# A two-layer trunk with eight experts: every second expert piece started by GpSimd's DMA queue, an over-capacity branch placed earlier, and the first pieces put in other tiles

## The chip, the cores and the metric

One core of a Trainium2 chip runs the whole program. The metric is the device time in microseconds (us) of one execution. The kernel before takes 1315.39 us (median of three runs, 1314.02 to 1319.24).

## The reference

A sequence of 256 tokens of width 1024 goes through two residual layers, each with two sub-layers of the form x <- LayerNorm(ALPHA * x + sublayer(x)). The first layer has a convolution and pooling mixer and a dense SwiGLU, the second a gated convolution with spatial gating and a top-2-of-8 expert SwiGLU. All tensors are float32. What matters here is the last sub-layer:

```python
def moe_swiglu(x, router, w_gate, w_up, w_down):
    t = x.reshape(-1, d)
    logits = (t @ router).astype(jnp.float32)
    top_logits, top_idx = lax.top_k(logits, TOP_K)          # 2 of 8
    top_w = jax.nn.softmax(top_logits, axis=-1)
    gates = jnp.sum(jax.nn.one_hot(top_idx, N_EXPERTS) * top_w[..., None], axis=1)
    out = jnp.zeros_like(t)
    for e in range(N_EXPERTS):
        out = out + gates[:, e:e + 1] * swiglu(t, w_gate[e], w_up[e], w_down[e])
    return out.reshape(bsz, s, d)
```

Each expert has w_gate and w_up of 1024 x 3584 and w_down of 3584 x 1024, so the eight experts are 352 MB of weights, all of which are read.

## The kernel before

**Pieces.** All large weights are cut into pieces (`chunks`) of 1 MiB each, in the order in which they are used. 57 pieces belong to the two layers' other matrices, 336 to the experts; this text counts the expert pieces from 0 to 335, so that piece m is chunk 57 + m. A piece is 512 rows of 512 columns for gate and up (2 KB runs) and 256 rows of 1024 columns for down (4 KB runs). The function `raw_half` starts a piece's DMA; it is called for half a piece at a time, ahead of its use, by `prep`. Every one of these DMAs is issued by SyncE (SP), at lines 123, 131, 133 and 136, in the order of the pieces.

**Tiles.** Normally a piece lands in one of eight `raw` tiles, which go round. A DMA waits in its queue until the last reader of its tile is done, and what stands behind it in the same queue waits too. For the first 60 expert pieces the table `AHEAD` gives further places: tiles of the earlier layers that are free by then ("fd" from piece 15 to 24, for instance; "fd" last holds the gains `rows` of the odd layer's first LayerNorm, which `affine` reads at lines 524 and 525). `IN_HI` and `IN_LO` put certain pieces in the tiles of the `hip` and `lop` pools, which otherwise hold converted halves: pieces 16 to 18 in `whi` and 19 and 20 in `wlo`, and, counted from the end, pieces 329 to 331 in `whi` and 332 and 333 in `wlo`.

**Passes.** The experts are ranked by their number of tokens, and eight passes p run over them, with room for 64, 160, 128, 128, 64, 64, 64 and 64 tokens (`CAPS`); pass 0 is always expert 0, the expert of the others is read into a register (`value_load`) once it is known. A pass has seven blocks f, each of a gate, an up and a down item; `plan` lists the 168 items of all passes, and an item uses two pieces. A narrow item (64 tokens) multiplies with the float32 piece as it landed. A wide item first splits each half into a rounded part (`whi`, ScalarE, line 151) and a rest (`wlo`, VectorE, line 158), from `hip` (6 tiles) and `lop` (5). Passes 0 alone, then 0 and 2, 2 and 6, 1 with 6, 4 and 5, 5 and 3, 3 and 7, and at last 7 alone run interleaved.

**The branch.** If an expert has more tokens than its room, `over_capacity` computes the rest in a loop; with these inputs the branch isn't taken. It stands `IF_AT` = 5 items before the last item (item 162, whose first piece is 324). Ahead of it `drain` works off all deferred steps, and `raw_half` starts all pieces that are left. SP, TensorE, ScalarE and VectorE have instructions in the branch, and each of them waits behind it for its own semaphores to reach the values that the branch leaves (line 1463).

**GpSimd's queue.** In program order behind the earlier layers' work it holds two DMAs of `rows` (line 529, for the tile "fd"), four multiplications `total` (line 1083), the branch, and two DMAs `lnf` of 512 KB each (line 1540). Expert piece 0 is started in program order ahead of `rows`, all others behind it.

**The end.** Item 167 uses pieces 334 and 335, whose DMAs are cut in two (`LAST_CUT`). Behind it stand the last combination, a LayerNorm and the store.

Of the kernel before, what the change touches and what calls it, by code (L numbers as in the profile page):

```python
# [8 lines left out]
F32 = mybir.dt.float32  # L9
# [8 lines left out]
P = 128  # L18
T = 256
# [4 lines left out]
NE = 8  # L24
# [8 lines left out]
RAW_BUFS = 8  # L33
WAIT = (6, 12, 6, 2)
CARRY = {(1, 0): 1, (1, 1): 2, (0, 0): 3, (0, 1): 3}
IF_AT = 5
CARRY_AT = 1
LAST_CUT = 2
AHEAD = {"ft": (0, 50), "fd": (15, 24), "fa": (2, 18), "fc": (3, 48), "fe": (7, 50), "fb": (8, 56), "f0": (9, 18), "f1": (10, 60)}

IN_HI, IN_LO = (16, 17, 18, -7, -6, -5), (19, 20, -4, -3)
TAIL, TAIL_HI, TAIL_LO = 12, 2, 1
RANK_AT = 3
FILL = (5, 2, 5, 4)
# [31 lines left out]
def tile_trunk(ctx: ExitStack, tc: tile.TileContext, a: dict, out: bass.AP, caps=CAPS, starts=STARTS,  # L76
               stop=None, dump=None):
    nc = tc.nc
    te, ve, se, pe_, sy = nc.tensor, nc.vector, nc.scalar, nc.gpsimd, nc.sync
# [21 lines left out]
    chunks, slot_pools = [], {"ra": rawp}  # L101
# [9 lines left out]
    def block_chunk(w, r0, c0):  # L111
        chunks.append((lambda: w[r0:r0 + 512, c0:c0 + 512].rearrange("(k p) f -> p k f", p=P), 4, 512))

    def raw_half(n):

        c, h = divmod(n, 2)
        src, k, f = chunks[c]
        if c in ahead and ahead[c] in ("whi", "wlo"):
            if c not in raws:
                pool = hip if ahead[c] == "whi" else lop  # L120
                raws[c] = [pool.tile([P, k // 2, f], F32, name=ahead[c]) for _ in range(2)]
                for i, r in enumerate(raws[c]):
                    sy.dma_start(r, src()[:, i * k // 2:(i + 1) * k // 2, :])
            return raws[c][h]
        if c not in raws:
            tag = ahead.get(c, "raw")
            raws[c] = slot_pools[tag[:2]].tile([P, k, f], F32, name="raw", tag=tag)
            v = src()
            if c < FIRST_CUT:
                for i in range(2):  # L130
                    sy.dma_start(raws[c][:, :, i * P:(i + 1) * P], v[:, :, i * P:(i + 1) * P])
            elif c < len(chunks) - LAST_CUT:
                sy.dma_start(raws[c], v)
            else:
                for i in range(2):
                    sy.dma_start(raws[c][:, i * k // 2:(i + 1) * k // 2, :], v[:, i * k // 2:(i + 1) * k // 2, :])
        return raws[c][:, :, h * P:(h + 1) * P] if k == DB else raws[c][:, h * k // 2:(h + 1) * k // 2, :]

    spare = []
# [59 lines left out]
    eid_reg = {}  # L199
# [61 lines left out]
        plan.insert(len(plan) - 2, plan.pop(len(plan) - 5))  # L261

    def expert(p, w, r0, nr, c0, ncol):
        def src():
            if p and p not in eid_reg:
                eid_reg[p] = sy.value_load(ctli[0:1, p:p + 1], min_val=0, max_val=NE - 1)
            if p == 0:
                v = w[0, r0:r0 + nr, c0:c0 + ncol]
            else:
                v = w[bass.ds(eid_reg[p], 1), r0:r0 + nr, c0:c0 + ncol].rearrange("o r f -> (o r) f")  # L270
            return v.rearrange("(k p) f -> p k f", p=P)
        chunks.append((src, nr // P, ncol))

# [8 lines left out]

    for tag, cs in (("whi", IN_HI), ("wlo", IN_LO)):
        for c in cs:
            ahead[c + (n_moe // 2 if c > 0 else len(chunks))] = tag

    def stay_warm(n, w, m=None):

# [1170 lines left out]
    def over_capacity():  # L1459
# [3 lines left out]
        with tc.If(flag > 0):  # L1463
# [15 lines left out]
            for e in range(NE):  # L1479
                with tc.For_i(0, FE, P) as f0:  # L1480
# [6 lines left out]
                    for i in range(2):  # L1487
                        for k in range(DB):
                            mm(bs[i][:, :T], wgu[:, i, k, :], xf[:, k, :], k == 0, k == DB - 1)
                    s = mop.tile([P, T], F32, name="fbh", tag="mh", bufs=2)  # L1490
                    se.activation(s, bs[0][:, :T], AF.Silu)
                    ve.tensor_tensor(s, s, bs[1][:, :T], op=OP.mult)
                    for t in range(2):
# [15 lines left out]
    for n, item in enumerate(plan):  # L1509
# [5 lines left out]
            later(1, gather, *gathers[item])  # L1515
        if n == end - IF_AT:
            drain()
            for c in range(made["hi"] // 2, len(chunks)):
                raw_half(2 * c)
            over_capacity()  # L1520
        if n == end - CARRY_AT:
# [93 lines left out]
```

## Time and profile before

| | |
|---|---|
| median of three runs | 1315.39 us |
| the profiled execution | 1314.88 us |
| its span in the trace | 1313.2 us |
| TensorE busy | 1256.2 us (96%) |
| VectorE, ScalarE, GpSimd busy | 713.5, 514.5, 32.0 us |
| moved by DMA | 421.17 MB, mean 321 GB/s |
| hardware queue, software queue | 414.58 MB, 5.28 MB |

Busy time of TensorE is modelled and isn't a measure of how close it is to its peak. The software queue is GpSimd's, the hardware queue SP's. "DMA share" in the views is the busy share of the 16 DMA engines; since packets overlap, it goes a little over 1.

### The profile page before, as it was taken

The numbers are of one execution on the slowest core, as the hardware profiler recorded it, in microseconds if no ns is written. First come the engines' busy times: TensorE is split into PE (matmuls) and PEld (weight loads), VectorE is DVE, ScalarE is ACT, GpSimd is POOL, SyncE is SP. The second block draws the span as 40 slices with busy tenths as digits, with TensorE's granted clock in tenths as the row PEclk, the third lists the DMA queues.
The fourth block names the chain that finished last, engine by engine and source line by source line (L and its number), as shares of the span: only waits on it lengthen the run. The fifth ranks groups of instructions, "written<-read, shape, count | busy, mean of one in ns | idle before, by whom it ended". The sixth has DMA issues, their size and how long they took to land. (4 is left out here: it accounts for less than half of the span.)

```text
span 1313.2 us, 19384 instructions
## 1 busy us (share of the span) xinstructions
PE 1256.2 (96%) x7585; PEld 871.1 (66%) x7585; DVE 713.5 (54%) x1105; ACT 514.5 (39%) x726; POOL 32.0 (2%) x69
## 2 busy tenths in 40 slices
PE   7989999999999999999999999999999999999875
PEld 6848888888777666667765566565556567665541
DVE  4897676667984244655534334434435565564313
ACT  4246555546442144544432233332333244454200
POOL 5000000001000001000000000000000000000000
PEclk8999999999999999999999999999999999999988
DMA  8425755176875999999999999999999999999991
GB/s 293 166 70 176 256 184 182 65 253 194 323 271 185 393 393 394 394 392 393 393 393 371 381 397 374 364 380 391 392 397 396 394 393 395 393 394 394 393 393 76
DMA packets 195884, 421.17 MB, mean 321 GB/s; under 512 B 6896, under 2 KB 43448, under 8 KB 195784
## 3 DMA queue, kind: packets, MB, share of 16 engines
q1 hardware_dynamic: 194280, 414.58, 85.2%
q0 software_dynamic: 1504, 5.28, 1.1%
q8 instruction: 61, 1.00, 0.3%
q14 instruction: 39, 0.32, 0.1%
HBM read 418.78 MB, written 1.05 MB: 320 GB/s over the span
## 5 line engine op out<-in xcount | busy, mean ns | idle before, releaser
L158 DVE TENSOR_TENSOR wlo<-raw,whi 128x1024 fp32r<-128x1024 f32 x354 | 417.8, 1220 | 175.8 <-ACT whi L151 159.1
L151 ACT ACTIVATE whi<-raw 128x1024 fp32r<-128x1024 f32 x354 | 354.6, 1050 | 215.7 <-DMA raw<-in_odd_moe_w_up 99.1
L98 PE MATMUL mm<-whi,xgw 128*128 128x512 f32 x672 | 215.9, 403 | 0.4 <-DVE total L1431 0.4
L98 PEld LDWEIGHTS mm<-whi,xgw 128*128 128x128 f32 x672 | 122.0, 189 | 44.6 <-issue 13.3
L98 PE MATMUL mm<-raw,f1k 128*64 128x256 f32 (+1 forms) x1344 | 133.9, 384 | 0.0
L98 PE MATMUL mm<-wlo,xgw 128*128 128x512 f32 x336 | 131.9, 392 | 0.3 <-DVE wlo L158 0.3
L98 PE MATMUL mm<-big,whi 128*128 128x512 f32 (+1 forms) x448 | 129.2, 368 | 2.5 <-ACT whi L151 1.8
L98 PE MATMUL mm<-raw,fek 128*64 128x256 f32 x880 | 106.6, 390 | 7.3 <-DVEq L1463 6.7
L98 PE MATMUL acc<-whi,mh 128*128 128x512 f32 x336 | 106.3, 397 | 1.7 <-ACT whi L151 1.7
L98 PEld LDWEIGHTS mm<-raw,f1k 128*64 128x64 f32 (+1 forms) x1344 | 72.7, 127 | 52.2 <-issue 17.4
L1298 ACT ACTIVATE fdk<-mm 128x256 f32<-128x256 f32 (+1 forms) x49 | 23.2, 474 | 182.1 <-PE mm L98 181.9
L98 PE MATMUL mm<-big,wlo 128*128 128x256 f32 x384 | 92.7, 283 | 0.0
L98 PEld LDWEIGHTS mm<-raw,fek 128*64 128x64 f32 x880 | 61.1, 139 | 45.5 <-issue 19.0
L1301 DVE TENSOR_TENSOR fdk<-mm,fdk 128x256 f32<-128x256 f32 (+1 forms) x49 | 26.3, 537 | 118.5 <-PE mm L98 118.5
L98 PEld LDWEIGHTS mm<-big,whi 128*128 128x128 f32 x448 | 74.9, 192 | 14.2 <-ACT whi L151 2.0
L98 PE MATMUL acc<-raw,fbs 128*64 128x512 f32 (+1 forms) x528 | 84.0, 507 | 0.0
L98 PEld LDWEIGHTS acc<-whi,mh 128*128 128x128 f32 x336 | 61.4, 188 | 24.4 <-ACT whi L151 11.0
L98 PEld LDWEIGHTS mm<-wlo,xgw 128*128 128x128 f32 x336 | 63.5, 189 | 14.9 <-DVE wlo L158 0.7
L98 PEld LDWEIGHTS mm<-big,wlo 128*128 128x128 f32 x384 | 69.3, 192 | 3.7
L98 PE MATMUL acc<-wlo,mh 128*128 128x512 f32 (+1 forms) x176 | 67.8, 401 | 0.5 <-DVE wlo L158 0.5
L98 PEld LDWEIGHTS acc<-raw,fbs 128*64 128x64 f32 (+1 forms) x528 | 26.6, 125 | 47.9 <-issue 44.9
L98 PE MATMUL acc<-whi,ffh 128*128 128x512 f32 x176 | 55.6, 396 | 0.0
(292 smaller groups left out, 1315.7 us busy)
## 6 DMA issues: line engine op xcount, KB each, us to landing
raw<-in_odd_moe_w_gate SPq DMA_DIRECT2D x110, 1024.0 KB, 13.8
raw<-in_odd_moe_w_up SPq DMA_DIRECT2D x109, 1024.0 KB, 13.9
raw<-in_odd_moe_w_down SPq DMA_DIRECT2D x105, 1024.0 KB, 12.8
raw<-in_even_ffn_w_gate SPq DMA_DIRECT2D x11, 1024.0 KB, 5.6
raw<-in_even_ffn_w_up SPq DMA_DIRECT2D x11, 1024.0 KB, 8.3
raw<-in_even_ffn_w_down SPq DMA_DIRECT2D x11, 1024.0 KB, 7.0
raw<-in_odd_w_in SPq DMA_DIRECT2D x10, 1024.0 KB, 15.2
raw<-in_even_w_in SPq DMA_DIRECT2D x5, 1024.0 KB, 8.8
```

Source lines behind the costliest of these rows:

```text
L98: te.matmul(o, lhsT, rhs, start=start, stop=stop)
L151: se.activation(his[n], r, AF.Copy)
L158: ve.tensor_tensor(los[n], r, his[n].bitcast(F32), op=OP.subtract)
L1298: se.activation(s, v, AF.Silu)
L1301: ve.tensor_tensor(s, v, s, op=OP.mult)
```

## The change

Five edits:

- A new function `raw_queue` gives the issuing engine of a piece: GpSimd for every second chunk of the experts, SP for the others. Since 57 chunks come before, GpSimd gets the expert pieces 0, 2, 4, ..., 334 and SP 1, 3, ..., 335. An item's two pieces so have one queue each. The register with the expert's number is loaded on both engines.
- `IF_AT` goes from 5 to 10: the branch stands before item 157 (piece 314).
- Ahead of the branch only pieces up to eight behind the present one are started, no longer all that are left; and no piece of the end goes to `whi` or `wlo` any more.
- At the start, pieces 15 to 17 go to `whi`, 18 and 19 to `wlo`, and 20 to "fd" (before: 15 to "fd", 16 to 18 to `whi`, 19 and 20 to `wlo`).
- A tile inside the branch has another tag ("sgate" in place of "mh").

```diff
-IF_AT = 5
+IF_AT = 10
-AHEAD = {"ft": (0, 50), "fd": (15, 24), ...
-IN_HI, IN_LO = (16, 17, 18, -7, -6, -5), (19, 20, -4, -3)
+AHEAD = {"ft": (0, 50), "fd": (20, 24), ...
+IN_HI, IN_LO = (15, 16, 17), (18, 19)
...
+    def raw_queue(c):
+
+        return pe_ if c >= n_moe // 2 and c % 2 else sy
...
+                v = src()
                 for i, r in enumerate(raws[c]):
-                    sy.dma_start(r, src()[:, i * k // 2:(i + 1) * k // 2, :])
+                    raw_queue(c).dma_start(r, v[:, i * k // 2:(i + 1) * k // 2, :])
...
             elif c < len(chunks) - LAST_CUT:
-                sy.dma_start(raws[c], v)
+                raw_queue(c).dma_start(raws[c], v)
...
     def expert(p, w, r0, nr, c0, ncol):
+        on = raw_queue(len(chunks))
+
         def src():
-            if p and p not in eid_reg:
-                eid_reg[p] = sy.value_load(ctli[0:1, p:p + 1], min_val=0, max_val=NE - 1)
+            if p and (p, on) not in eid_reg:
+                eid_reg[p, on] = on.value_load(ctli[0:1, p:p + 1], min_val=0, max_val=NE - 1)
...
-            ahead[c + (n_moe // 2 if c > 0 else len(chunks))] = tag
+            ahead[n_moe // 2 + c] = tag
...
-                    s = mop.tile([P, T], F32, name="fbh", tag="mh", bufs=2)
+                    s = mop.tile([P, T], F32, name="fbh", tag="sgate", bufs=1)
...
-            for c in range(made["hi"] // 2, len(chunks)):
+            for c in range(made["hi"] // 2, state["use"] // 2 + RAW_BUFS):
                 raw_half(2 * c)
             over_capacity()
```

## Rows read from the trace of the kernel before

**Rows 1.** Windows of the streaming stage: busy us (instructions) per engine, granted clock, DMA share, GB/s.
```profile
430.00:460.00 30.00, 30.00 (x212) 18.11 (x209) 8.01 (x12) 6.13 (x9) 0.00 (x0) 1.00 1.04 393
...
1100.00:1200.00 100.00, 99.99 (x554) 67.36 (x550) 55.56 (x61) 44.80 (x54) 0.00 (x0) 1.00 1.04 393
```
**Rows 2.** Waits: engine, tile, line, released by: us in total, times, longest.
```profile
ACT whi L151 <- DMA raw<-in_odd_moe_w_up: 99.1, 33, 9.8
```
**Rows 3.** Windows around the start of the expert stage.
```profile
380.00:390.00 10.00, 9.84 (x43) 7.64 (x42) 7.70 (x19) 1.26 (x3) 0.00 (x0) 1.00 1.01 374
390.00:400.00 10.00, 10.00 (x68) 8.85 (x67) 6.31 (x25) 4.98 (x11) 0.00 (x0) 1.00 0.83 314
400.00:410.00 10.00, 10.00 (x80) 8.23 (x79) 5.40 (x25) 3.09 (x7) 0.00 (x0) 1.00 0.00 0
410.00:420.00 10.00, 10.00 (x92) 6.47 (x92) 6.66 (x17) 1.16 (x3) 0.00 (x0) 1.00 0.51 185
```
**Rows 4.** Timeline of SP's DMA queue there: start us, us, what, count.
```profile
343.93 1.64 SPq L133 DMA_DIRECT2D raw<-in_odd_moe_w_up  x2
...
384.77 29.32 SPq L133 DMA_DIRECT2D raw<-in_odd_moe_w_down  x2
414.18 2.09 SPq L123 DMA_DIRECT2D whi<-in_odd_moe_w_gate  x4
```
**Rows 5.** Timeline of VectorE and TensorE: last readers of the tiles.
```profile
413.00 0.69 DVE L525 TENSOR_TENSOR tok<-tok,rows 128x512 f32<-128x512 f32 x1
402.78 0.72 PE L98 MATMUL acc<-whi 128*128 128x512 f32 x2
```
**Rows 6.** Timeline of GpSimd.
```profile
304.15 0.77 POOL L901 DMA_DIRECT2D fc<-in_odd_sgu_w  x1
...
375.62 0.56 POOL L529 DMA_DIRECT2D rows<-in_odd_ln_g  x1 [61.11 <-DVE big L436]
...
509.92 5.89 POOL L1083 TENSOR_SCALAR total<-tok 128x512 f32<-128x512 f32 x4 [133.21 <-DVE wlo L158]
992.51 0.59 POOL L1540 DMA_DIRECT2D lnf<-in_odd_ln_g  x1 [476.70 <-PE mm L98]
```
**Rows 7.** Timeline of TensorE and ScalarE: the first items of the expert stage.
```profile
406.94 2.81 PE L98 MATMUL mm<-raw,xg 128*64 128x256 f32 x24
448.69 3.89 ACT L151 ACTIVATE whi<-raw 128x1024 fp32r<-128x1024 f32 x4
...
462.17 3.89 ACT L151 ACTIVATE whi<-raw 128x1024 fp32r<-128x1024 f32 x4
```
**Rows 8.** Page, DMA issues: count, KB each, median us to landing.
```profile
raw<-in_odd_moe_w_gate SPq DMA_DIRECT2D x110, 1024.0 KB, 13.8
```
**Rows 9.** One window and one VectorE instruction beside GpSimd's DMAs.
```profile
990.00:1000.00 10.00, 10.00 (x85) 6.62 (x84) 3.65 (x9) 0.98 (x2) 1.12 (x2) 1.00 1.04 391
375.37 1.22 DVE L158 TENSOR_TENSOR wlo<-raw,whi 128x1024 fp32r<-128x1024 f32 x1
```
**Rows 10.** Windows in which the DMA rate sinks.
```profile
700.00:800.00 100.00, 96.50 (x706) 58.58 (x707) 40.91 (x52) 29.68 (x38) 0.00 (x0) 1.00 1.02 383
800.00:900.00 100.00, 99.22 (x718) 60.48 (x718) 40.45 (x51) 31.22 (x43) 0.00 (x0) 1.00 1.00 373
```
**Rows 11.** The branch: TensorE's loads behind it, SP's semaphores behind it, a window.
```profile
1268.22 0.32 PEld L98 LDWEIGHTS mm<-raw,fek 128*64 128x64 f32 x4 [7.15 <-issue]
L1463 SPq EVENT_SEMAPHORE  x8: 17/17/17, 1282.6 to 1286.8; - x8
1260.00:1270.00 10.00, 3.25 (x17) 1.80 (x15) 1.49 (x3) 0.39 (x1) 0.00 (x0) 0.81 1.05 390
```
**Rows 12.** TensorE's last item.
```profile
1293.39 3.60 PE L98 MATMUL acc<-raw,fbs 128*64 128x512 f32 x16
```
**Rows 13.** Page, DMA queues: packets, MB, share of 16 engines' span.
```profile
q1 hardware_dynamic: 194280, 414.58, 85.2%
q0 software_dynamic: 1504, 5.28, 1.1%
```

More of the change, by code (lines that the diff above doesn't have):

```diff
@@ L35 @@
 CARRY = {(1, 0): 1, (1, 1): 2, (0, 0): 3, (0, 1): 3}
-IF_AT = 5
+IF_AT = 10
 CARRY_AT = 1
 LAST_CUT = 2
-AHEAD = {"ft": (0, 50), "fd": (15, 24), "fa": (2, 18), "fc": (3, 48), "fe": (7, 50), "fb": (8, 56), "f0": (9, 18), "f1": (10, 60)}
-IN_HI, IN_LO = (16, 17, 18, -7, -6, -5), (19, 20, -4, -3)
+AHEAD = {"ft": (0, 50), "fd": (20, 24), "fa": (2, 18), "fc": (3, 48), "fe": (7, 50), "fb": (8, 56), "f0": (9, 18), "f1": (10, 60)}
+IN_HI, IN_LO = (15, 16, 17), (18, 19)
 TAIL, TAIL_HI, TAIL_LO = 12, 2, 1
@@ L132, in raw_half @@
             elif c < len(chunks) - LAST_CUT:
-                sy.dma_start(raws[c], v)
+                raw_queue(c).dma_start(raws[c], v)
             else:
                 for i in range(2):
-                    sy.dma_start(raws[c][:, i * k // 2:(i + 1) * k // 2, :], v[:, i * k // 2:(i + 1) * k // 2, :])
+                    raw_queue(c).dma_start(raws[c][:, i * k // 2:(i + 1) * k // 2, :],
+                                           v[:, i * k // 2:(i + 1) * k // 2, :])
         return raws[c][:, :, h * P:(h + 1) * P] if k == DB else raws[c][:, h * k // 2:(h + 1) * k // 2, :]
@@ L269, in src @@
             else:
-                v = w[bass.ds(eid_reg[p], 1), r0:r0 + nr, c0:c0 + ncol].rearrange("o r f -> (o r) f")
+                v = w[bass.ds(eid_reg[p, on], 1), r0:r0 + nr, c0:c0 + ncol].rearrange("o r f -> (o r) f")
             return v.rearrange("(k p) f -> p k f", p=P)
```

## The prediction, before the changed kernel ran

> **What bounds the kernel now.** First the windows. From 430 to about 1283 us the DMA engines are busy without a gap (share 1.04) and move 393 GB/s [rows 1]. An expert piece of 1.049 MB so takes 2.67 us, and 336 of them 897 us, most of the span. The waits say the same from the reader's side: ScalarE's conversion of up pieces alone waited 33 times, 99 us in all, for a DMA [rows 2]. So in this stage time is bytes over rate, and a change gains only by moving bytes into stretches where the engines idle, by closing a hole in the stream, or by shortening what follows the last byte. The views that matter are therefore the two ends of the stream and its holes.
>
> **The start.** Between 380 and 420 us the rate is 374, 314, 0 and 185 GB/s [rows 3]. Against 393 these four windows leave (19 + 79 + 393 + 208) / 393 x 10 = 17.8 us unused. SP's queue shows why: its down pieces 14 and 15 begin at 384.77 and fill the time to 414.1, and only at 414.18 come the `whi` pieces [rows 4]. Piece 15 goes into "fd", whose last reader is the `affine` that ends at 413.00 + 0.69 = 413.69 us [rows 5]; pieces 16 to 20 stand behind it in the queue though their tiles are free sooner.
>
> In the change pieces 15 to 19 need `whi` and `wlo` tiles only. The last reader of those is the warming matmul that ends at 402.78 + 0.72 = 403.5 us [rows 5], most others are done before. So up to five pieces, 13.3 us of transfers, can run in the unused stretch, and only piece 20 waits for 413.69, on GpSimd, with SP's odd pieces free to go on.
>
> Something is given back. GpSimd has piece 0 and then, in program order, the two `rows` DMAs, which waited for their tile until 375.62 [rows 6]; all other even pieces stand behind them. SP now begins pieces 2 and 3 at 343.93 and 4 and 6 behind them, well ahead of 14 at 384.77 [rows 4]; in the change 2, 4 and 6 start about 377, three pieces x 2.67 = 8.0 us that move into the stretch. They are still in time: TensorE begins piece 0 at 406.94 [rows 7], 30 us later. Net 17.8 - 8.0 = **9.8 us** more of the stream is done by 420.
>
> It counts only if TensorE can keep up. From piece 0 (406.94) to the first conversion, piece 24 (448.69), it takes 1.74 us a piece, and from piece 24 to piece 30 (462.17) 13.48 / 6 = 2.25 us [rows 7]; both are under 2.67. The lead of 9.8 us on the DMA side is made good at 0.42 us a piece, so within 24 pieces more, before the extra tiles of `AHEAD` end at piece 60. Bounds: 0 if TensorE never catches up, 13.3 if all five pieces count. I take 9.8.
>
> **The stream itself.** One queue already fills the engines, so I take no gain from a second and no loss. The nearest row for GpSimd's queue beside a full SP queue is `lnf`: two DMAs of 512 KB from 992.51 on [rows 6], and the window 990 to 1000 has 391 GB/s [rows 9], as the rest. Issuing costs GpSimd 0.77 us for 512 runs against 0.56 for 128 [rows 6], on an engine that has almost nothing else to do; 168 pieces in 900 us are one in 5.3 us. A few tenths later per piece are hidden, since a piece is issued 13.8 us before it lands [rows 8], five pieces' worth. `total` now holds GpSimd's queue until 509.92 [rows 6], but it waits for piece 47's split, about when the next pieces' tiles come free too: 0.
>
> The Trainium skill has a rule against the software path (DMA: Bandwidth & Descriptors, section SWDGE vs HWDGE vs iDMA): GpSimd writes its descriptors into SBUF, and VectorE locks it out during its two-port modes. In this trace the `rows` DMA of 375.62 took 0.56 us [rows 6] in the middle of a `wlo` subtraction that ran from 375.37 to 376.59 [rows 9], so no lock shows for this form, and by the row nothing is added; by the rule every issue could slip by one such 1.22 us, which the 13.8 us ahead would hide as well.
>
> Holes: 700 to 900 us run at 383 and 373 GB/s [rows 10], (10 + 20) / 393 x 100 = 7.6 us lost to waits for tiles. Two queues neither add tiles nor free them sooner. I take 0, between -7.6 (all closed) and +7.6 (an item's two pieces now land together, tiles are held longer, the holes double).
>
> **The branch and the end.** TensorE stands still for 7.15 us behind the branch and resumes at 1268.22; the window has 32% busy and a granted clock of 0.81 [rows 11], a mix of the two levels, 2.4 and 1.2 GHz, after that idling. From there it works without a break until 1293.39 + 3.60 = 1296.99 [rows 12]: 28.8 us for the last six items. But SP passes the semaphore of its last piece at 1286.8 [rows 11], 10.2 us earlier. So at the very end TensorE is late, by the branch: without the stop it would end at 1289.8, and the data would allow 1286.8 plus a quarter of the last item (3.60 / 4 = 0.9). I take the 7.15 us, rounded **7.1**.
>
> Is the stop hidden in its new place? Eleven items, 22 pieces, follow it: 58.7 us of transfers. TensorE needs 28.8 for the last six, four narrow items x 3.5 = 14.0 and one wide one: of the 13.48 us of [rows 7], four narrow pieces are 7.0, the wide item 6.5. With the stop that is 56.4 us, 2.3 under 58.7. It fits, barely. Bounds: 0 to 9.2 (10.2 - 0.9).
>
> Behind the branch SP waits for its semaphores, eight of them, one after the other until 1286.8 [rows 11]; it had nothing left to start, now it has the odd pieces from 323 on. It must first let its outstanding ones land: with eight pieces outstanding on both queues, up to 21.4 us. GpSimd has no instruction in the branch and no such wait, so its queue goes on with 322, 324 and 326 as tiles come free, and one queue is enough for the engines. I take 0; if GpSimd's pieces wait for tiles during TensorE's stop, up to 7.15 us of stream are lost.
>
> Last, an item's two pieces run at half rate side by side, and the second half of the last but one no longer lands ahead of the last: up to two quarters more of the last item behind the last byte, 1.8 us. I add **2 us** for this and for small gaps at the branch.
>
> **Sum.** 1314.88 - 9.8 - 7.1 + 2.0 = 1300.0 for the profiled execution, whose span of 1313.2 leaves 1.7 us around it. The median of the runs is 0.5 us above that execution: **1300.5 us**.
>
> **Rivals.**
> *The lead is lost* (0.18). TensorE runs close to the DMA's pace, and in 700 to 900 it is the slower [rows 10]. If the early lead comes to nothing, the end alone counts: 1315.4 - 7.1 + 2 = 1310.3; if it is halved, about 1305.
> *The software queue is slower per byte* (0.14), the one that ends on the other side. The page has 85.2% for 414.58 MB, 0.2055% per MB, and 1.1% for 5.28 MB [rows 13]; with its rounding, 1.05 to 1.15, this is 0.199 to 0.218 per MB, so at most 6% dearer. Half of the stream, 168 pieces or 448 us of transfers, would then cost 27 us more: 1327.5. It decides from 448 x 0.033 = 14.9 us, that is from 3.3% per byte, and gives slower by over 0.5% (6.6 us) from 4.8%. For it speaks that only 1504 such packets were seen; against it, the 391 GB/s with 1 MB of them [rows 9]. A page of the Trainium skill would have it so: DMA: Bandwidth & Descriptors, section Latency and other measured facts, says that engines 7 and 15 are usually slower, with descriptor fetches of the software path as its best guess; no view here shows single engines.
> *The end gets a new hole* (0.10). The stop holds back tiles, GpSimd's next pieces wait for them, SP still drains: 7.15 us are lost and the end gains nothing: 1315.4 - 9.8 + 7.15 + 2 = 1314.8, no change.
> *The second queue closes the holes* (0.08): 1300.5 - 7.6 = 1293.
>
> **How the numbers follow.** The forecast itself has 0.50, with 1293 to 1308 as its own range. Within 0.5%, about what can be told from no change, is 1308.8 to 1322. Faster: 0.50, 0.08 and two thirds of the lost lead, 0.12: 0.70. Same: 0.06, 0.10 and a small part of the slower queue: 0.18. Slower: 0.12. The range reaches from 1288 (13.3 at the start, 9.2 at the end and part of the holes) to 1317, which leaves out the slower queue and little else.
>
> **What would show it.** Right: no 0 GB/s window around 400 us; pieces 15 to 19 issued before 404; 393 GB/s from then to the end with GpSimd's queue holding about 176 MB; TensorE's stop at about 1220 and its last matmul within 3 us of the last landing. Wrong: a rate in the stream under 390 with both queues full, packets of the software queue above the other's share per MB, ScalarE's waits for DMA gone while TensorE runs on (the lead is lost), or SP's semaphores behind the branch with a rate that sinks.

## The result and the profile after

| | before | after |
|---|---|---|
| median, us | 1314.0 | 1321.9 |
| range of the runs, us | 1312.7 to 1319.2 | 1319.7 to 1329.9 |
| ratio to before, 95% interval | | 1.0061 (1.0041 to 1.0082) |
| span of the profiled execution, us | 1313.2 | 1325.0 |
| mean granted clock | 0.987 | 0.981 |

The changed kernel is 0.6% slower; the forecast was 1300.5 us, 1% faster. The profiled execution of after lies some 5 us above its median, so a loss read from its trace is a little too large.

The start did what was forecast, and more. The windows around the start and where the `AHEAD` tiles end, kernel after (busy us and instructions of PE, PEld, DVE, ACT, POOL, then granted clock, DMA share, GB/s):

```profile
380.00:390.00 10.00, 9.82 (x48) 7.82 (x47) 7.08 (x19) 1.82 (x3) 2.83 (x4) 1.00 1.03 390
390.00:400.00 10.00, 10.00 (x66) 8.84 (x65) 6.37 (x30) 4.23 (x10) 0.71 (x1) 1.00 1.03 397
400.00:410.00 10.00, 10.00 (x85) 7.94 (x85) 5.89 (x22) 3.66 (x9) 0.00 (x0) 1.00 1.03 392
410.00:420.00 10.00, 10.00 (x92) 6.43 (x90) 5.32 (x15) 0.58 (x2) 2.66 (x4) 1.00 1.03 395
...
530.00:540.00 10.00, 10.00 (x56) 8.47 (x55) 3.68 (x4) 2.31 (x4) 0.54 (x1) 1.00 0.84 306
540.00:550.00 10.00, 10.00 (x62) 5.56 (x61) 4.42 (x4) 6.38 (x9) 2.25 (x3) 1.00 0.64 231
```

The stretch that had 0 and 185 GB/s [rows 3] is full. Counted in bytes moved, from the DMA records of both traces, after is 14.5 us ahead of before when 100 MB are in. In the last two lines (87 + 162) / 393 x 10 = 6.3 us of it are given back: the tiles are full, TensorE is busy in every microsecond, and the transfers have to wait. At 200 MB, around 715 us, 1.8 us of the lead are left.

Then the stream. Windows of 100 us of after:

```profile
700.00:800.00 100.00, 92.94 (x658) 56.25 (x656) 35.09 (x44) 28.97 (x38) 12.84 (x18) 0.97 0.98 361
800.00:900.00 100.00, 97.96 (x703) 58.99 (x704) 41.78 (x54) 31.53 (x43) 12.56 (x17) 0.98 0.95 353
1100.00:1200.00 100.00, 95.36 (x524) 66.20 (x524) 55.56 (x60) 43.18 (x52) 13.21 (x18) 0.98 1.00 380
```

Before had 383 and 373 GB/s in the first two [rows 10] and 393 in the third, with TensorE busy 99.99 of 100 [rows 1]. Both sink together: TensorE stands still 7.1 us in the first window (3.5 before), and later the transfers do too. The page of after tells what the two queues did (part 3: packets, MB, share of the 16 engines; part 6: count, KB each, median us from issue to landing):

```profile
q1 hardware_dynamic: 119784, 238.41, 49.6%
q0 software_dynamic: 47248, 181.45, 36.2%
...
raw<-in_odd_moe_w_gate POOLq DMA_DIRECT2D x55, 1024.0 KB, 9.8
raw<-in_odd_moe_w_gate SPq DMA_DIRECT2D x55, 1024.0 KB, 13.3
raw<-in_odd_moe_w_up SPq DMA_DIRECT2D x55, 1024.0 KB, 13.5
raw<-in_odd_moe_w_up POOLq DMA_DIRECT2D x55, 1024.0 KB, 10.0
raw<-in_odd_moe_w_down POOLq DMA_DIRECT2D x55, 1024.0 KB, 10.0
raw<-in_odd_moe_w_down SPq DMA_DIRECT2D x54, 1024.0 KB, 8.0
```

GpSimd's queue is not dearer by the byte: 36.2 / 181.45 = 0.200% per MB against 49.6 / 238.41 = 0.208%. But of gate and up, a piece of SyncE's takes 3.5 us longer to land than one of GpSimd's. (The page's median for SyncE rests on an eighth of its landings. Over all pieces from 60 to 309, worked from the landing records, SyncE's take 14.5, 12.6 and 10.7 us for gate, up and down, GpSimd's 9.7, 10.0 and 9.9; so the page's 8.0 us for SyncE's down pieces is not typical.) The packets differ too. GpSimd's 176 MB of expert pieces came in 45744 packets (both lines less the 1504 packets and 5.28 MB of [rows 13]), 3.85 KB each; SyncE's whole queue has 2.0 KB on the mean. One by one, the DMA records have 4096 bytes for GpSimd's packets, whatever the piece, and for SyncE's 2048 bytes in gate and up pieces and 4096 in down pieces; beside these each transfer has 16 packets of 4 bytes, which lower the means.

What that does is seen around piece 152, where TensorE stands still longest in the first window. Issue and landing in us, worked from the records of both traces; even pieces are GpSimd's in after:

```
piece              152    153    154    155    156    157    158    159
before, issued    778.2  779.9  781.8  787.6  789.5  791.2  792.9  795.0
before, landed    790.4  793.1  795.8  798.5  801.2  803.9  806.6  809.3
after, issued     780.2  781.7  783.0  789.4  791.5  792.9  794.9  796.4
after, landed     791.5  798.3  795.6  805.1  800.4  807.8  804.5  813.1
```

Before, they land in their order, 2.7 us apart. After, 154 lands before 153 and 156 before 155; 153, which is needed next, is 5.2 us later than before. ScalarE's and TensorE's timeline of after there (start us, us, instruction, in brackets the idle time before it and what ended it):

```profile
791.57 2.00 ACT L157 ACTIVATE whi<-raw 128x1024 fp32r<-128x1024 f32 x2 [9.16 <-DMA raw<-in_odd_moe_w_up]
798.45 2.00 ACT L157 ACTIVATE whi<-raw 128x1024 fp32r<-128x1024 f32 x2 [4.87 <-DMA raw<-in_odd_moe_w_up]
...
792.74 3.62 PE L98 MATMUL mm<-raw,fek 128*64 128x256 f32 x32
801.15 0.69 PE L1316 MATMUL mm<-ident,fdk 128*128 128x128 f32 x2 [4.79 <-DVE fdk L1309]
```

ScalarE converts the two halves of piece 152 at 791.57 and then waits for 153 until 798.45. VectorE makes the `fdk` that TensorE needs only behind its own work on 153, so TensorE runs dry for 4.79 us while piece 154 lies in its tile and 156 arrives. When the late pieces are in, all tiles are full, TensorE has to catch up, and the transfers wait in turn.

At the branch TensorE's weight loads, SyncE's semaphores and the windows of after read:

```profile
1256.19 0.33 PEld L98 LDWEIGHTS mm<-raw,fek 128*64 128x64 f32 x4 [7.10 <-issue]
...
L1471 SPq EVENT_SEMAPHORE  x8: 17/17/17, 1254.9 to 1258.3; - x8
...
1250.00:1260.00 10.00, 3.77 (x18) 2.49 (x20) 0.00 (x0) 0.00 (x0) 0.00 (x0) 0.57 0.69 269
1260.00:1270.00 10.00, 9.75 (x65) 6.76 (x62) 5.30 (x6) 4.17 (x5) 2.27 (x3) 0.92 0.84 288
```

The stop is as long as before, 7.10 against 7.15 us [rows 11], with the granted clock down to 0.57 in the window of the stop, mostly the lower level of 1.2 GHz; now it stands earlier. But the rate, 390 in the window of the stop before, is 269 and 288: (124 + 105) / 393 x 10 = 5.8 us of stream. This hole in the transfers is not what the end waits for. TensorE's last item of the experts is

```profile
1303.49 5.37 PE L98 MATMUL acc<-raw,fbs 128*64 128x512 f32 x24
```

From the loads at 1256.19 to its end TensorE waits 0.3 us in all, and the last piece lands at 1303.7, 5 us before that item ends.

### The profile page after: what moved, and what is told of

The parts are those of the page before. It is cut to its first block, busy times and chain, and to the rows that moved or that the text cites. A ratio compares the mean times of both kernels' runs of the same rounds, so it can differ in the third digit from the quotient of the medians.

```text
span 1325.0 us, 19425 instructions
## 1 busy us (share of the span) xinstructions
PE 1261.0 (95%) x7585; PEld 874.4 (66%) x7585; DVE 714.3 (54%) x1105; ACT 511.6 (39%) x726; POOL 158.7 (12%) x240
## 3 DMA queue, kind: packets, MB, share of 16 engines
q1 hardware_dynamic: 119784, 238.41, 49.6%
q0 software_dynamic: 47248, 181.45, 36.2%
## 5 line engine op out<-in xcount | busy, mean ns | idle before, releaser
L98 PE MATMUL mm<-whi,xgw 128*128 128x512 f32 x672 | 219.6, 409 | 0.0
L98 PE MATMUL acc<-whi,mh 128*128 128x512 f32 (+1 forms) x344 | 108.2, 402 | 0.0
L98 PE MATMUL acc<-raw,fbs 128*64 128x512 f32 (+1 forms) x560 | 91.8, 512 | 0.0
L98 PEld LDWEIGHTS acc<-whi,mh 128*128 128x128 f32 (+1 forms) x344 | 61.9, 187 | 23.8 <-ACT whi L157 10.4
L138 POOL DMA_DIRECT2D raw<-in_odd_moe_w_down x55 | 39.2, 712 | 283.9 <-PE mm L98 223.4
L138 POOL DMA_DIRECT2D raw<-in_odd_moe_w_up x55 | 41.8, 759 | 251.9 <-PE mm L98 175.2
L138 POOL DMA_DIRECT2D raw<-in_odd_moe_w_gate x55 | 41.4, 753 | 225.0 <-PE mm L98 121.4
## 6 DMA issues: line engine op xcount, KB each, us to landing
raw<-in_odd_moe_w_gate SPq DMA_DIRECT2D x55, 1024.0 KB, 13.3
```

The lines of the kernel that those rows point to most:

```text
L98: te.matmul(o, lhsT, rhs, start=start, stop=stop)
L138: raw_queue(c).dma_start(raws[c], v)
```

## The experiments

Times are medians beside the kernel before on the same chip (its median there 1314.6 to 1315.5 us), with the ratio to it and its 95% interval. **Theory A** at the outset: the change loses because the two queues share the engines unevenly, so that pieces land out of order, and because TensorE has no time to spare, so that neither a lead nor a late piece is made good. **Rivals**: the moved branch and first pieces cost (B); the second queue costs nothing (the prediction's step).

### One part at a time

The queue alone (`e1_queue_only`): after, with `IF_AT`, `AHEAD`, `IN_HI`, `IN_LO`, the branch's loads and `fbh` as before.

> Only the second queue: every second piece of the experts is begun by GpSimd, while the first pieces, the tiles of the stream's end and the branch are those of the kernel before. Theory A (the two queues share the 16 engines by packets; GpSimd's packets of gate and up are about twice as long as SyncE's, so later pieces land before earlier ones, tiles are held, and a TensorE that is itself near its limit stands still in longer lumps): the whole loss of the changed kernel's stream is here, +11 to +18 us, 1325 to 1332 us. Rival B (the second queue costs nothing by itself, the loss comes from the moved branch and first pieces): 1313 to 1316 us. Rival C (the prediction's step, no change of rate and no other cost): 1314 us as well, with windows of the stream as before.

The moves alone (`e2_moves_only`): after, with

```diff
-        return pe_ if c >= n_moe // 2 and c % 2 else sy
+        return sy
```

> All pieces stay with SyncE; only the moves are made: the three first pieces are issued earlier, the branch stands where the changed kernel has it, with its tiles. Theory A: the start gives 1 to 4 us (the transfers run ahead by 10 to 14 us, but TensorE had been the later of the two there), the stream goes as before, the end gives 5 to 7 us less some 3 us in which SyncE empties its queue at the branch: 1305 to 1309 us. Rival B (the moves are what costs): 1318 to 1325 us. By the prediction's own sum for these two parts, 9.8 - 8.0 + 8 us kept at the start and 7.1 us at the end: 1297 to 1301 us.

The first pieces alone (`e3_first_only`): before, with

```diff
-AHEAD = {"ft": (0, 50), "fd": (15, 24), ...
+AHEAD = {"ft": (0, 50), "fd": (20, 24), ...
-IN_HI, IN_LO = (16, 17, 18, -7, -6, -5), (19, 20, -4, -3)
+IN_HI, IN_LO = (15, 16, 17, -7, -6, -5), (18, 19, -4, -3)
```

> The kernel before with the three first pieces issued earlier and nothing else. By the prediction's step (the lead of 9.8 us at the start is kept to the end) 1304 us. By theory A (the matmuls of the first hundred pieces take all of their time already, so a lead of the transfers of 10 to 14 us gives them only 1 to 3 us) 1311 to 1313 us. If the held tiles make a new wait at the end of the early pieces: 1314 to 1317 us.

| run | us | ratio |
|---|---|---|
| the queue alone | 1327.4 | 1.0087 (1.0055 to 1.0119) |
| the moves alone | 1308.6 | 0.9947 (0.9931 to 0.9964) |
| the first pieces alone | 1313.6 | 0.9980 (0.9969 to 0.9990) |

The whole loss is the queue's, 11.9 us by itself and 1321.9 - 1308.6 = 13.3 us on top of the moves (15 by the two ratios, whose bases differ by 1.5 us). The moves gain 6.9 us: 2 to 3 by the start, the other 4 to 5 by the end, which is a difference, since no run has the end alone. B falls, and so do the prediction's 9.8 us for the start. Windows of the run with the first pieces alone:

```profile
430.00:460.00 30.00, 30.00 (x204) 18.22 (x200) 8.01 (x12) 6.12 (x9) 0.00 (x0) 1.00 1.01 376
...
530.00:540.00 10.00, 10.00 (x55) 8.48 (x55) 3.66 (x4) 2.31 (x4) 0.00 (x0) 1.00 0.81 294
540.00:550.00 10.00, 10.00 (x62) 5.55 (x61) 4.45 (x4) 6.40 (x9) 0.00 (x0) 1.00 0.71 253
```

With one queue, too, 6 us of the lead (14.9 us in bytes at 100 MB) are given back at 530 to 550 us, while TensorE is busy in every microsecond; at 200 MB 2.0 us are left. The conversions of piece 110 and the next pieces, which ScalarE makes behind its work on TensorE's results, say what TensorE made of it (duration min/median/max, first and last start), before:

```profile
L151 ACT ACTIVATE whi<-raw x4: 1041/1042/1046, 680.6 to 683.5; 128x1024 fp32r<-128x1024 f32 x4
```

and with the first pieces alone:

```profile
L151 ACT ACTIVATE whi<-raw x5: 1041/1045/1057, 677.2 to 685.6; 128x1024 fp32r<-128x1024 f32 x5
```

They are 3.4 us earlier at 680, of which 1.4 were there at the first conversion already (447.3 against 448.69 [rows 7]). So with the pieces there ahead of time (110 landed at 667.7) the 86 pieces from the first conversion to this one still took 677.2 - 447.3 = 229.9 us, 2.67 us a piece. In the kernel before, they took 680.6 - 448.7 = 231.9 us, 2.70 us a piece, and TensorE was busy in all of it but 1.7 us, as the window of before over this stretch shows:

```profile
448.70:680.60 231.90, 230.16 (x1344) 155.67 (x1342) 118.83 (x128) 99.25 (x123) 5.89 (x4) 1.00 1.04 393
```

### TensorE given time to spare

Does the lead last if TensorE can follow? Three kernels leave out the third of the three matmuls in the experts of 128 rows: before (`e7_before_two`), after (`e8_after_two`) and the moves alone (`e10_moves_two`).

```diff
-                wm(bs[bi], l[:, 0:P], l[:, P:2 * P], w[0][:, j, :], w[1][:, j, :], k == 0, k == DB - 1)
+                wm2(bs[bi], l[:, 0:P], l[:, P:2 * P], w[0][:, j, :], w[1][:, j, :], k == 0, k == DB - 1)
...
+    def wm2(o, lh, ll, wh, wl, start, stop):
+        mm(o, lh, wh, start, False)
+        mm(o, ll, wh, False, stop)
```

> The kernel before, with the third of the three matmuls (activations by the rounded rest of the weights) left out in the experts of 128 rows; conversions and transfers stay. It takes some 504 matmuls of 0.39 us, 196 us, from TensorE, so that the transfers alone set the stream. Theory A: some stalls of the transfers that TensorE caused go, 1290 to 1308 us. The run is there as the base for the next one.

> The changed kernel with the same third matmul left out in the experts of 128 rows. Theory A (the start lead was lost, and the late halves cost, because TensorE had no time to spare): with time to spare the transfers' lead of 10 to 14 us should last to the end and the late halves should cost little, so that it is 8 to 18 us faster than the kernel before with the same part left out. Rival B (the second queue slows the transfers themselves or holds them by its own waits): no faster than that one, or slower by up to 8 us.

> The moves alone (all pieces with SyncE), with the third matmul of the experts of 128 rows left out. The changed kernel with that part left out ran 14 us ahead of the kernel before until 700 us and then lost it in holes of the transfers between 700 and 830 us and between 1100 and 1160 us, although TensorE had time to spare. Theory A1 (the holes come from the two queues): with one queue the lead that the earlier first pieces give is kept to the end; the stream is full at 393 GB/s, 4 to 10 us under the 1310.3 us of the kernel before with that part left out by the start and 4 more by the end: 1296 to 1304 us. Rival B1 (any lead is lost in those stretches, since the tiles there come free by TensorE's order and not by the transfers'): 1305 to 1309 us, with the holes at 800 us and 1110 us as with two queues.

| run | us | ratio to before with all matmuls |
|---|---|---|
| before, two matmuls | 1310.3 | 0.9962 (0.9948 to 0.9976) |
| after, two matmuls | 1320.4 | 1.0036 (1.0013 to 1.0058) |
| moves alone, two matmuls | 1292.3 | 0.9821 (0.9801 to 0.9840) |

Before gains only 4.5 us (its mean granted clock is 0.948 then), less than was expected: there the transfers set the stream. (TensorE's busy time falls by 1256.2 - 1187.2 = 69 us; the expectation's 196 added up single matmuls, which overlap.) The moves alone now gain 1310.3 - 1292.3 = 18.0 us, more than was expected, so the lead at the start is worth all of its 14 us, beside what the end gives, as soon as TensorE can follow it. That half of theory A stands. The other half, that the late pieces cost little once TensorE has time, fell: after is 28 us behind the moves alone (17 in the profiled executions). Windows of after with two matmuls:

```profile
430.00:700.00 270.00, 247.41 (x1470) 155.00 (x1468) 138.75 (x156) 111.27 (x140) 41.93 (x51) 0.94 1.02 386
700.00:830.00 130.00, 111.89 (x837) 65.28 (x834) 48.68 (x60) 40.06 (x55) 17.78 (x24) 0.92 0.96 358
...
785.00:790.00 5.00, 0.00 (x0) 0.00 (x0) 0.00 (x0) 0.63 (x1) 0.00 (x0) 0.59 1.03 386
...
800.00:805.00 5.00, 5.00 (x43) 3.54 (x39) 4.19 (x8) 3.87 (x6) 0.00 (x0) 1.00 0.71 234
805.00:810.00 5.00, 4.84 (x44) 3.46 (x48) 2.58 (x4) 2.05 (x4) 0.70 (x1) 1.00 0.62 219
```

The same two long windows of the moves alone with two matmuls:

```profile
430.00:700.00 270.00, 250.13 (x1512) 155.61 (x1510) 139.63 (x159) 114.56 (x143) 5.99 (x4) 0.97 1.04 391
700.00:830.00 130.00, 121.65 (x880) 69.94 (x877) 54.56 (x66) 41.24 (x55) 0.00 (x0) 0.95 1.03 389
```

After keeps a lead of 14 us over the kernel before to 700 us and then loses it. From 785 to 790 TensorE has nothing to do at all, with the engines moving 386 GB/s; then, from 800 on, TensorE is full and the rate falls to 234 and 219. In this execution piece 153 landed at 789.3, behind 154 (784.9) and 156 (789.1); with one queue it landed at 776.6. So the stalls and the holes come from the order of landing and not from TensorE's load.

### Why the order is lost

Two explanations were left. **P**: the engines serve the two queues packet by packet, and GpSimd's packets of gate and up are twice as long as SyncE's, so that its pieces get more of the rate. **Q**: two queues, each waiting for tiles in its own order, lose the order whatever their packets. Five runs on the queue alone, or the changed kernel, tried to part them from the side of the pieces: GpSimd's gate and up pieces cut in four (`e5_short_packets`), only down pieces by GpSimd (`e6_down_only`), only up pieces (`e11_up_only`), the halves exchanged (`e12_queue_other`, and on the changed kernel `e13_after_other`). Their expectations still call P theory A; Q is the rival that speaks of two queues.

```diff
 e5
-                raw_queue(c).dma_start(raws[c], v)
+                if k == 4 and raw_queue(c) is pe_:
+                    for i in range(k):
+                        pe_.dma_start(raws[c][:, i:i + 1, :], v[:, i:i + 1, :])
+                else:
+                    raw_queue(c).dma_start(raws[c], v)
 e6 (e11 with "u")
-        return pe_ if c >= n_moe // 2 and c % 2 else sy
+        m = c - n_moe // 2
+        return pe_ if m >= 0 and c % 2 and plan[m // 2][0] == "d" else sy
 e12, e13
-        return pe_ if c >= n_moe // 2 and c % 2 else sy
+        return pe_ if c >= n_moe // 2 and c % 2 == 0 else sy
```

> The run with the queue alone, but GpSimd begins each of its gate and up pieces as four transfers of one run of rows each (256 KB, 2 KB in a row), so that its packets may come out as short as SyncE's 2 KB. If they do (the trace's queue table tells the mean packet), theory A (unequal shares by packet size spoil the order) expects GpSimd's and SyncE's pieces to take about the same time to land, and the loss of 11.9 us of the queue alone to go for the most part: 1314 to 1320 us. Rival B (the loss comes from something else of the second queue: GpSimd's waits in order, two transfers in flight at once): 1324 to 1332 us. If the packets stay at 4 KB: as the queue alone, 1324 to 1330 us.

> The queue alone, but GpSimd begins only every second down piece, whose rows are 4 KB long on either queue; all gate and up pieces stay with SyncE. Theory A (unequal packets): with equal packets in two thirds of the shared stretches less, at most a third of the loss stays: 1314 to 1319 us. Rival B (two queues at once spoil the order, whatever the packets): 1319 to 1323 us, since the down pieces are a third of all. Rival C (the second queue costs by its mere presence): 1325 us or more.

> The queue alone, but GpSimd begins only every second up piece: as many transfers as in the run with the down pieces, but of rows of 2 KB, which SyncE's queue moves in packets of 2 KB and GpSimd's in packets of 4 KB. Theory A (unequal packets spoil the order): GpSimd's up pieces land some 3 us sooner than SyncE's, and this third of the pieces costs a third to a half of the 11.9 us, 1318 to 1321 us, where the down pieces cost nothing (1314.0 us). Rival B (two queues on a third of the pieces cost nothing, whichever they are; it takes all of them): 1313 to 1316 us.

> The queue alone with the halves exchanged: SyncE begins the first piece of each item, GpSimd the second. Theory A (GpSimd's faster pieces land before the pieces that are needed first): now the faster queue has the half that is issued and needed last, so that both halves of an item land together and the next item's first piece isn't ahead of this one's second: most of the 11.9 us goes, 1314 to 1320 us. Rival B (what costs is two queues that wait in their own order for tiles, whichever has which half): 1324 to 1331 us.

> The changed kernel, branch and first pieces moved, with the halves exchanged as in the run before this one. The moves were worth 6.9 us with one queue. Theory A: 1307 to 1314 us, near the run with the moves alone (1308.6 us). Rival B: as the changed kernel, 1319 to 1325 us.

| run | us | ratio |
|---|---|---|
| gate and up cut in four | 1332.0 | 1.0129 (1.0106 to 1.0153) |
| down alone | 1314.0 | 0.9991 (0.9977 to 1.0004) |
| up alone | 1316.4 | 1.0003 (0.9987 to 1.0019) |
| halves exchanged | 1321.7 | 1.0064 (1.0040 to 1.0089) |
| halves exchanged, with the moves | 1318.2 | 1.0022 (1.0000 to 1.0044) |

The first told nothing: GpSimd's 181.5 MB came in 52576 packets in place of 47248, but the new ones are packets of 4 bytes, 16 for each of the added transfers; the others have 4096 bytes as before, so they had not been shortened as meant. Down alone cost nothing, as P had it; but up alone cost nothing either, where P had 3 to 6 us, so with a third of the pieces the two can't be told apart. Exchanging the halves saved 5.7 and, with the moves, 3.7 us by the medians, less than P had and more than Q. The median landing of the page was again sooner on GpSimd's queue for gate and up, 10.4 against 14.2 and 9.8 against 13.7 us, so the inversion had only changed sides.

The next four runs made SyncE's packets longer instead. Gate and up pieces are read as rows of 4 KB from the down weights (same bytes, other data), with one queue and with two, with and without the third matmul (`e14_moves_two_rows4`, `e15_after_two_rows4`, `e16_moves_rows4`, `e17_after_rows4`).

```diff
+        if ncol == 512:
+            w, r0, nr, c0 = md, c0 + r0 // 2, 256, 0
...
+    def wide_rows(t):
+        return t.rearrange("p (k a) f -> p k (a f)", a=2) if wide_on[0] and t.shape[2] == 512 else t
...
+        wide_on[0] = c >= n_moe // 2 and k == 4
...
-                raw_queue(c).dma_start(raws[c], v)
+                raw_queue(c).dma_start(wide_rows(raws[c]), v)
```

> The moves alone on one queue, the third matmul of the experts of 128 rows left out, and the experts' gate and up pieces read from the down weights (same bytes, 128 rows by 4 KB twice, in place of four times 2 KB; other data, so another result). The base for the next run. Both theories: about as with rows of 2 KB, 1292.3 us, or up to 10 us less if longer packets move faster: 1282 to 1294 us.

> The same with the two queues. Theory P (unequal packets): both queues now move packets of 4 KB, share evenly and keep the order, so the 28 us between one queue and two (1320.4 against 1292.3 us) go: 0 to 8 us above the run before this. Rival Q (two queues each waiting for tiles in their own order): the gap stays, 18 to 30 us above the run before this.

> The moves alone on one queue with all matmuls, gate and up pieces read as rows of 4 KB from the down weights (other data). Base for the next run: 1298 to 1310 us.

> The changed kernel with all matmuls, gate and up pieces read as rows of 4 KB from the down weights (other data). Theory P: the 13.3 us between the moves alone and the changed kernel go for the most part, 0 to 4 us above the run before this. Rival Q: they stay, 9 to 15 us above it.

| | one queue (moves alone), us | two queues (changed), us | difference |
|---|---|---|---|
| rows of 2 KB, all matmuls | 1308.6 | 1321.9 | 13.3 |
| rows of 4 KB, all matmuls | 1302.8 | 1304.6 | 1.8 |
| rows of 2 KB, two matmuls | 1292.3 | 1320.4 | 28.1 |
| rows of 4 KB, two matmuls | 1265.4 | 1270.1 | 4.8 |

Queue lines and landings of the page, two queues with rows of 4 KB and all matmuls:

```profile
q1 hardware_dynamic: 91112, 238.41, 48.4%
q0 software_dynamic: 47248, 181.45, 35.7%
...
raw<-in_odd_moe_w_down POOLq DMA_DIRECT2D x165, 1024.0 KB, 11.0
raw<-in_odd_moe_w_down SPq DMA_DIRECT2D x164, 1024.0 KB, 10.7
```

SyncE's packets for the same 238.41 MB fell from 119784 to 91112: 28672 fewer, 256 for each of its 112 gate and up pieces, which is 512 of 2 KB against 256 of 4 KB. GpSimd's stay at 47248. With equal packets the landings are equal, 11.0 and 10.7 us, and 13.3 us of loss shrink to 1.8, 28.1 to 4.8.

The records of the packets and landings show the share and the order themselves. The second and third columns take those microseconds between 430 and 1190 us (72, 143, 108 and 242 of them) in which each queue had at least two pieces issued over 2.5 us before and not landed, its two oldest from gate or up. The last column takes pieces 40 to 319 and counts how often, of two in a row, the later landed first.

| two queues | GB/s, GpSimd and SyncE | GpSimd's share | inverted, of 279 |
|---|---|---|---|
| rows of 2 KB, all matmuls (changed) | 236, 150 | 61% | 73 |
| rows of 2 KB, two matmuls | 247, 139 | 64% | 98 |
| rows of 4 KB, all matmuls | 212, 197 | 52% | 6 |
| rows of 4 KB, two matmuls | 203, 205 | 50% | 0 |

With one queue none is inverted. So P stands: the queue with the longer packets got more of the rate, and with equal packets two queues that wait for tiles in their own order kept the order, which Q denied. What is left of the difference, 2 to 5 us, may have another cause, and the runs don't tell. The number of inversions alone does not give the loss: the runs with a third of the pieces had 27 (down) and 35 (up) and lost nothing, and the exchanged halves 80. The Trainium skill has the rule behind it (DMA: Bandwidth & Descriptors, section Queues, rings and completion order): an engine goes round the queues that have work and takes a whole packet from each. With packets of 4 and 2 KB that would be two thirds and one third of the rate; the 61% and 64% above come near it, and the 52% and 50% with equal packets agree.

### Where the second queue could still be of use

Two runs looked for a place for it at the branch, where SyncE's queue is emptied: GpSimd for odd expert pieces from 306 on only (`e4_late_queue`), and GpSimd for down pieces only, with the moves (`e18_moves_down`).

```diff
 e4
-        return pe_ if c >= n_moe // 2 and c % 2 else sy
+        return pe_ if c >= n_moe // 2 + 306 and c % 2 else sy
 e18
-        return pe_ if c >= n_moe // 2 and c % 2 else sy
+        m = c - n_moe // 2
+        return pe_ if m >= 0 and c % 2 and plan[m // 2][0] == "d" else sy
```

> The moves, and GpSimd's queue only for the odd pieces from expert piece 306 on, the last twenty pieces or so before the branch; all earlier ones by SyncE. Theory A: the order of landing is spoilt for twenty pieces instead of three hundred, so the loss of the stream goes (some 1 us is left of it), and the second queue covers the time in which SyncE's queue is emptied at the branch, some 2 us: 1303 to 1308 us. If the second queue costs where the branch is (its own drain beside SyncE's): 3 to 8 us above the run with the moves alone, 1310 to 1315 us.

> The changed kernel with GpSimd beginning only every second down piece (4 KB packets on both queues); gate and up pieces stay with SyncE. Theory P (unequal packets cost, a second queue by itself costs next to nothing): as the moves alone, 1308.6 us, within 2 us, or up to 3 us less if its pieces fill the hole at the branch: 1305 to 1311 us. Rival Q (a second queue costs where the branch is, as in the run with the late pieces only, 1311.2 us, or by its own order): 1311 to 1318 us.

They took 1311.2 us (0.9961, 0.9946 to 0.9976) and 1315.4 us (1.0003, 0.9985 to 1.0020), 2.6 and 6.8 us more than the moves alone. In both the loss of the profiled execution lies behind the branch: piece 322 lands at 1252.5 us in the moves alone, and at 1250.3 and 1251.4 in these two, so up to there they are no later. Windows of the moves alone:

```profile
1240.00:1250.00 10.00, 9.92 (x68) 6.45 (x64) 3.73 (x4) 4.17 (x5) 0.00 (x0) 0.83 0.57 204
...
1270.00:1280.00 10.00, 10.00 (x75) 4.93 (x72) 1.00 (x3) 0.38 (x1) 0.00 (x0) 1.00 1.03 407
```

and of the moves with GpSimd's down pieces:

```profile
1240.00:1250.00 10.00, 10.00 (x68) 6.66 (x65) 2.81 (x3) 4.17 (x5) 0.00 (x0) 0.76 0.58 209
...
1270.00:1280.00 10.00, 7.67 (x66) 4.33 (x62) 0.85 (x2) 0.38 (x1) 2.14 (x4) 1.00 1.03 405
```

The hole at the branch is there either way (204 and 209 GB/s). At 1270 to 1280 TensorE waits: piece 329, the second half of the last up item and SyncE's, landed at 1277.4 instead of 1272.9, because GpSimd's down piece 330, issued later, overtook it (1271.6). A down piece of 4 KB packets beside up pieces of 2 KB ones is the same fault again; the expectation from `e6_down_only`, that down pieces are free, did not hold there. With the late queue 329 landed at 1279.6, behind 330 at 1272.7.

The version that beats both kernels is the one with the moves alone, 1308.6 us, with no second queue.

## Why the prediction was wrong, point by point

| term of the sum | forecast, us | measured, us | from |
|---|---|---|---|
| the start | -9.8 | -2 to -3 | first pieces alone |
| the branch and the end | -7.1 | -4 to -5 | moves alone less first pieces alone |
| the second queue in the stream | 0 (-7.6 to +7.6) | +13 to +15, under 1 of it at the end | after less the moves alone |
| last landing, small gaps | +2.0 | not told apart | |

**What bounds the kernel: half right, and the fault began here.** The DMA engines are full in the two windows of [rows 1] (not "without a gap" from 430 to 1283: [rows 10] have 383 and 373 GB/s); but the same two rows show TensorE busy 30.00 of 30.00 and 99.99 of 100. Two resources were at their limit, and I read one. With the third matmul out of the wide experts, before gained only 4.5 us, so the transfers do set its pace; the moves alone went from 1308.6 to 1292.3, so as soon as the transfers ran ahead, TensorE set it.

**The start: the lead came, its worth was wrong.** There is no window near 0 GB/s, and the lead is even larger, 14.5 us by bytes: the even pieces behind `rows` put after 2.7 us behind at 80 MB, where the prediction had given back 8.0. The step that failed is that TensorE can keep up and makes the lead good within 24 pieces. I took 1.74 and 2.25 us a piece from two stretches of 42 and 13 us at the beginning of the stage, where narrow experts are frequent; over the next 86 pieces it was 2.70 us, with TensorE busy throughout, against 2.67 for the transfers. The lead could not be made good at 0.42 us a piece, nor at all: with the pieces there early it was still 2.67. So the rival "the lead is lost" (0.18) was the right one here, with its reason. That the lead counts in full once TensorE is lighter, the run of 1292.3 us shows.

**The stream: this term of 0 turned the gain into a loss.** That one queue fills the engines already, so that a second brings neither gain nor loss, is right of the rate: between 430 and 1230 us the windows of 10 us with a DMA share of 1.03 or more have 391.8 GB/s on the mean in after and 392.2 in before, and the share per MB is no higher. It missed that bytes per us are not all: which bytes come first counts too. The nearest row taken, `lnf` beside a full SP queue at 391 GB/s [rows 9], is blind to order. The row that bore on it was in front of me: [rows 13] have 5.28 MB in 1504 packets, 3.5 KB each, for the one queue, and 414.58 MB in 194280, 2.1 KB each, for the other. The bound of +7.6 us named an effect that came, tiles held longer and larger holes, and about half of its size; but it had an item's two pieces landing together, while in after the second lands behind the next item's first.

**The rival "software queue slower per byte"** gave 1327.5 us, the only one on the slow side and close to what came; but its mechanism did not happen. By the two lines of the page the price per MB is 0.200% for GpSimd's queue and 0.208% for SyncE's.

**The branch and the end: some 60 to 70% of the size, by another mechanism.** TensorE's stop moved to 1249 and is 7.10 us long as before, but it is not hidden: behind it TensorE works without a break to the end of the last item, and the last piece lands 5.2 us before that in after (1303.7 and 1308.9) and 3.1 in the moves alone (1288.2 and 1291.3). The step that failed is "It fits, barely": the prediction had 49.3 us of work behind the stop, and with the stop 56.4 against 58.7 of transfers; the moves alone took 1291.3 - 1239.0 = 52.3, and with the stop of 6.9 us 59.2. Most of what the end gained was something else: in the 60 us up to the end of the last item TensorE stood still 10.5 us with the first pieces alone, the stop and over 3 us of waits, and 7.5 with the moves, where few waits are left beside the stop. TensorE's first loads and last matmuls behind the stop, in the moves alone:

```profile
1239.00 0.33 PEld L98 LDWEIGHTS mm<-raw,fek 128*64 128x64 f32 x4 [6.92 <-issue]
...
1285.93 5.37 PE L98 MATMUL acc<-raw,fbs 128*64 128x512 f32 x24
```

The hole that I had put at 0 came too: with SyncE letting its pieces land behind the branch (semaphores until 1258.3) the rate fell to 269 and 288 GB/s, and GpSimd's queue did not cover it, since it waited for tiles that TensorE, standing still, had not given back: 12.5 us in its longest wait there. The bound of 7.15 us for this case held; 5.8 us of transfers were lost. With one queue the hole is about as large, 204 GB/s in one window, (393 - 204) / 393 x 10 = 4.8 us. But in neither does the end wait for it, since TensorE is the later one. The second queue's loss is there ahead of the branch: TensorE resumes at 1256.2 in after and at 1239.0 in the moves alone, 17.2 us apart, and the two profiled spans differ by 17.7.

**The signs named at the end of the prediction** read well: "a rate in the stream under 390" (361, 353, 380), "SP's semaphores behind the branch with a rate that sinks", "ScalarE's waits for DMA gone while TensorE runs on" (none of its conversions between 440 and 500 us waited for one; two did before). Each was put down as a way to be wrong and each happened.

## What to carry to other kernels

Before a transfer stream is given a lead, look at TensorE's busy share in the same windows: where both are full, a lead is worth only what the slower one leaves over, and the pace has to be read over as many pieces as the lead must last. Two DMA queues that feed one consumer in turn kept their order here only with packets of equal length; otherwise the queue with the longer ones brought first what was needed later. So compare packets and MB of each queue in the page, and the time from issue to landing of each, before halving a stream between them. A transfer or an engine's stop that is shortened or moved helps only if the work that ends last was waiting for it: read which one that is behind the stop. A part of a change that costs can hide one that gains: run each part alone, and keep the one that gains (here the moves, 1308.6 us).

## What the runs showed of the hardware that was not expected

- SyncE's queue moves a row of 2 KB as one packet of 2048 bytes, GpSimd's joins rows into packets of 4096: 47248 packets on its queue whether the rows were of 2 or of 4 KB.
- While both queues had gate and up pieces under way, the one with packets of 4096 bytes got 61 to 64% of the rate against packets of 2048, and 50 to 52% against packets of 4096.
- The stream was faster with rows and packets of 4 KB. Full slices of the page have 393 or 394 GB/s with gate and up in rows of 2 KB and 409 with rows of 4 KB; here that was 27 us with two matmuls (1292.3 to 1265.4), and 6 with all three, where TensorE is the limit.
- Issuing costs GpSimd little: 0.70 to 0.81 us a piece. Cutting its gate and up pieces into four transfers left the packets at 4096 bytes; that run took some 5 us more than the queue alone, with intervals that overlap a little.
- Two queues of unequal packets also spread the times: the runs with the halves exchanged range over 14 us (1317.1 to 1331.1), those of the kernel before over 6.6 and those of the moves alone over 4.
- The branch that isn't taken costs TensorE most: its COMPARE_BRANCH took 6.24 us in before and after, against 0.05 to 0.07 us on the other engines.
